# Placing TensorE's weight operands by their byte address modulo 128 in a one-core encoder layer

## Chip, cores, metric

The kernel runs on one core of a Trainium2 chip, as a single launch. The metric is device time in microseconds, the median of three runs. Work is spread over the engines TensorE (PE; its weight loads are listed apart, as PEld), VectorE (DVE), ScalarE (ACT), GpSimd (POOL) and the DMA queue of SyncE (SP).

## What is computed

One layer of a hybrid encoder, for 512 positions of 1024 channels in float32. One projection feeds eight differential attention heads and a bidirectional Mamba-2 scan of 16 heads in four groups; both results are concatenated and projected back, and a SwiGLU block follows, each with a residual and a layer norm:

```python
h = jnp.einsum('bsd,de->bse', x, w_in[l])
q, k, v, z, xbc, dt_raw = jnp.split(h, splits, axis=-1)
attn_out = diff_attention(q, k, v, ...)
ssd_out = ssd_mixer(z, xbc, dt_raw, ...)
mix = jnp.einsum('bse,ed->bsd', jnp.concatenate([attn_out, ssd_out], axis=-1), w_out[l])
x = layernorm(DEEPNORM_ALPHA * x + mix, ln1_g[l], ln1_b[l])
hid = jax.nn.silu(jnp.einsum('bsd,df->bsf', x, w_gate[l])) * jnp.einsum('bsd,df->bsf', x, w_up[l])
ffn = jnp.einsum('bsf,fd->bsd', hid, w_down[l])
x = layernorm(DEEPNORM_ALPHA * x + ffn, ln2_g[l], ln2_b[l])
```

## The kernel before

Every large product is made in three float32r products: each operand is split into a rounded part `h` and a remainder `l`, and `mm3` (L174 to L179) adds h·h, h·l and l·h in one PSUM bank. `product` (L883 to L887) does the same in the gate and up stage. In a call `T.matmul(o, a, b)` the operand `a` is **stationary** (128 columns, loaded into the array ahead of the matmul: the PEld row) and `b` is **moving** (256 or 512 columns, streamed through it).

**The weight chunks.** The weights lie in HBM as 130 chunks of [128, 1024] float32. `wload` (L96) fetches a chunk by DMA into a tile of tag `raw`; `wprep` (L101) makes its parts, `h` on ACT (L106) and `l` on DVE (L107), in tiles `wh` and `wl` of the pool `wp`, which has three buffers a tag. `wget` (L110) calls it two chunks ahead. Chunks 0 to 23 are the scan's projections in four groups of six (the last two of six are z), 24 to 47 the attention's in four groups of six (the first two are v), 48 to 63 the output projection (`I_OUT`), 64 to 107 gate and up (`I_FF`), 108 to 129 down (`I_DN`).

**Stages in order of time, by the trace.** Scan projections and scan (to about 220 us): `col_units` (px, pB, pC: weights stationary, 512 columns of x moving) and `row_units` (z: x stationary, 256 columns of weights moving). Attention (about 220 to 450 us): q and k by `col_units`, v by `row_units`, woven between the steps of the heads by hand-written counts. Output projection `wo` (to about 528 us; 512 columns of weights moving, the mix tiles stationary); its last four chunks are kept in tiles `hold` of the pool `hw` by `tile_major` (L764). Gate and up: the first tiles whole (`ff_mm`, 256 columns), then Winograd's 2 x 2 form over 20 pairs (about 553 to 747 us): of its seven products of 12 matmuls the two of `p_1` and `p_2` have a weight chunk's own tiles `wh`, `wl` as stationary operands (rows `M<-x1h,wh` and `C<-x1h,wh`), the other five have sums and parts that `halves` makes in the pool `fp` (S1 to S4, A22). Down projection `dn` (to the end): weights moving, the split `hid` tiles (`hid_split`, L1006) stationary; its last sequence tile goes in two banks of 256 columns, `dn13x` and `dn13ps`, and its last four chunks are kept in tiles `keep`, in the place of x.

Order on each engine is the order of the code, with a few pieces held back by `tc.issue_after`; a tile's next use waits until its readers are done.

**Where operands lie.** Every row of an operand that a matmul uses begins at the tile's byte address in the partition plus a multiple of 128 bytes, so the address modulo 128 is the same for all slices of a tile. In the built program it is 96 for x, x1, T1 to T3, mix and all `wh`, `wl`; 32 for S1 to S4, A22 and `hold`; `keep` has 96; the split `hid` tiles have 96 in three rotating buffers (`dnr`) and 32 in the pool `dn` and in the first tile. 'Near' below means that the two operands of a matmul have the same address modulo 128, 'far' that they differ by 64.

Of the kernel before, what the change touches and what calls it, by code (L numbers as in the profile page):

```python
# [8 lines left out]
F32 = mybir.dt.float32  # L9
R32 = mybir.dt.float32r  # L10
# [3 lines left out]
P = 128  # L14
# [14 lines left out]
I_OUT = N_IN  # L29
I_FF = I_OUT + 16  # L30
I_DN = I_FF + 2 * FT
# [19 lines left out]
def encoder(ctx, tc, xt, xs, wall, wdt, consts, masks, vecs, pvec, lnv, out):  # L51
# [21 lines left out]
    def weave(steps, units, counts):  # L73
        """Emits steps in order with counts[i] of the units after step i, and the remaining units at the end."""
        done = 0
        for f, n in zip(steps, counts, strict=True):
            f()
            for u in units[done:done + n]:
                u()
            done += n  # L80
        for u in units[done:]:
            u()

# [1 line left out]
    cst = cp.tile([P, N_C], F32, name="cst")  # L85
# [6 lines left out]

    wcache = {}
    AHEAD = 2

    def wload(i):  # L96
# [4 lines left out]
    def wprep(i, raw=None, h=None, l=None):  # L101
        raw = wload(i) if raw is None else raw
        if h is None:
            h = wp.tile([P, 1024], R32, tag="wh", name=f"wh{i}")
            l = wp.tile([P, 1024], R32, tag="wl", name=f"wl{i}")
        A.copy(h, raw)  # L106
        V.tensor_tensor(l, raw, h.bitcast(F32), op=ALU.subtract)  # L107
        wcache[i] = (h, l)
# [6 lines left out]

# [1 line left out]
    xh = xtp.tile([P, KT, S], R32, tag="xh", name="xh")  # L117
# [63 lines left out]
    def col_units(i, name, done, step=2):  # L181
        """x @ w for 128 columns, transposed: [columns, 512]; then done(psum)."""
        st = {}

        def unit(k0):
            if k0 == 0:
                st["o"] = bank("mm", name)
                st["w"] = [w.rearrange("p (k c) -> p k c", k=KT) for w in wget(i)]
            h, l = st["w"]
            mm3(st["o"], [(h[:, k], l[:, k], xh[:, k], xl[:, k]) for k in range(k0, k0 + step)],  # L190
                first=k0 == 0, last=k0 + step == KT)
            if k0 + step == KT:
                done(st["o"])
        return [lambda k0=k0: unit(k0) for k0 in range(0, KT, step)]

    def row_units(i, name, tag, done):
        """x @ w for 256 columns: two banks of [128 positions, 2, 256]; done(half, psum)."""
        st = {}

        def unit(tp, tt, kh):  # L200
            if (tp, tt, kh) == (0, 0, 0):
                w0, w1 = wget(i, 2), wget(i + 1, 1)
                st["w"] = [[w.rearrange("p (k c) -> p k c", k=4) for w in ww] for ww in (w0, w1)]
            if (tt, kh) == (0, 0):
                st["o"] = bank(tag, f"{name}{tp}")
            t = 2 * tp + tt
            sl = slice(t * P, (t + 1) * P)
            h, l = st["w"][kh]
            mm3(st["o"][:, tt * 256:(tt + 1) * 256],
                [(xh[:, 4 * kh + k, sl], xl[:, 4 * kh + k, sl], h[:, k], l[:, k]) for k in range(4)],  # L210
                first=kh == 0, last=kh == 1)
            if (tt, kh) == (1, 1):
                done(tp, st["o"])
        return [lambda a=(tp, tt, kh): unit(*a) for tp in range(2) for tt in range(2) for kh in range(2)]

# [1 line left out]
    sps = ExitStack()  # L217
# [27 lines left out]

# [1 line left out]
    dtv = ep.tile([P, 2, NT, NH], F32, name="dtv")  # L247
# [4 lines left out]
    sel = msk[:, M_SEL:M_SEL + 256].rearrange("p (a k) -> p a k", a=2)  # L252
    # per direction d: rows erow[d] carry the exponents, the other 64 rows the mask
    erow = (slice(0, 64), slice(64, 128))
# [115 lines left out]

    # stationary parts of the exponents per direction and half of the columns, in the last mix tiles' places
    lhsC = [[mxp[0].tile([P, NT, P], R32, tag=f"m{q}{14 + d}", name=f"lhsC{d}{q}") for q in "hl"] for d in range(2)]
# [6 lines left out]

    # mix^T in two float32r parts: 16 tiles of [128 channels, 512]  # L380
    mixh, mixl = [None] * 16, [None] * 16
# [6 lines left out]

# [1 line left out]
    bc = lambda a, n: a[:, :, None].broadcast_to([a.shape[0], 4, n])  # L390
# [124 lines left out]

# [1 line left out]
    va, qk = {}, {}  # L517
# [31 lines left out]

# [1 line left out]
    late = []  # L551
# [18 lines left out]

# [1 line left out]
    mxp[0] = mxs.enter_context(tc.tile_pool(name="mxa", bufs=1, side="right"))  # L572
# [72 lines left out]

# [1 line left out]
    def pair(i, ahead=None):  # L647
        return [w.rearrange("p (k c) -> p k c", k=2) for w in wget(i, ahead)]

    def outer_units(i0, order, lhs, acc, n0, n1, total):  # L650
        """acc(t) += lhs tiles (pairs in order) x weight chunks i0 + n0 .. i0 + n1 - 1."""
        st = {}

        def unit(c, i):
            if i == 0:
                st["w"] = pair(i0 + c)
            h, l = st["w"]
            eh, el = lhs(2 * order[c] + i)
            for t in range(NT):
                sl = slice(t * P, (t + 1) * P)  # L660
                for b, o, w in acc(t):
                    mm3(b, [(eh[:, sl], el[:, sl], h[:, i, o:o + w], l[:, i, o:o + w])],
                        first=c == 0 and i == 0, last=c == total - 1 and i == 1)
        return [lambda c=c, i=i: unit(c, i) for c in range(n0, n1) for i in range(2)]
# [34 lines left out]

# [1 line left out]
    fx = ctx.enter_context(tc.tile_pool(name="fx", bufs=1))  # L701
    xr = fx.tile([P, NT, D], F32, tag="res", name="xr")

    def ln_consts(pool, i):
        r = []
        for j in (i, i + 1):
            r.append(pool.tile([P, D], F32, tag=f"ln{j}", name=f"ln{j}"))
            nc.gpsimd.dma_start(r[-1], lnv[j][None, :].broadcast_to([P, D]))  # L708
        return r
# [54 lines left out]
    def tile_major(i0, order, lhs, acc, done, hold, after):  # L764
        """As outer_units, with the last NHELD chunks resident and used one sequence tile at a time."""
        n = len(order)
# [21 lines left out]
    acc1 = [[(bank("ps", f"wo1{t}"), 0, 512)] for t in range(NT)]  # L788
    with tc.tile_pool(name="hw", bufs=1) as hw:
        ln1 = ln_consts(hw, 0)  # L790
        tile_major(I_OUT + 8, OUT_ORDER, mix, acc1.__getitem__, done1,
                   lambda j: [hw.tile([P, 1024], R32, tag=f"{q}{j}", name=f"hold{q}{j}") for q in "hl"],
                   lambda: wget(I_FF))
    mxs.close()

# [1 line left out]
    hidp = ctx.enter_context(tc.tile_pool(name="hid", bufs=1, side="right"))  # L797
# [11 lines left out]

    # Winograd's 2 x 2 form: operands from x1^T's blocks B (k half, sequence half)  # L810
    def block(i, j):
# [16 lines left out]
    def t_steps(q):  # L828
        """x1^T of sequence tile 2 + q, and the operands that come of it."""
        b12, b22 = x1t(2 + q, 0), x1t(2 + q, 1)  # L830
# [12 lines left out]

    # operands from the weight blocks of two column tiles: A11 A12 / A21 A22 (columns, k half)
    ops, mats = {}, {}
# [50 lines left out]
    def put(j, f, c, src):  # L896
        """One block of gate (silu) or up (times gate) into hid."""
        d = hid_tile(f)[:, c]
        if j % 2 == 0:
            A.activation(d, src, AF.Silu)  # L900
        else:
            V.tensor_tensor(d, d, src, op=ALU.mult)
# [42 lines left out]

    # the first two tiles of gate and up, whole; sequence half 0 of three chunks first
    def ff_w(f, w):
# [50 lines left out]

# [1 line left out]
    NEARLY = 1  # L1000
# [5 lines left out]
    def hid_split(e, ph):  # L1006
        """hid tile e in two parts; the later tiles' parts stay for both column halves."""
        key = e if e >= NRING else (ph, e)
# [39 lines left out]
    ffs.close()  # L1048
    dn = ctx.enter_context(tc.tile_pool(name="dn", bufs=1))
    ln2 = ln_consts(dn, 2)  # L1050
    for f in units[NMORE:]:
# [93 lines left out]
```

## Time and profile before

| | |
|---|---|
| median of 3 runs | 878.93 us (878.69 to 879.1) |
| span of the profiled execution, first to last instruction | 876.8 us |
| mean granted TensorE clock over the span | 0.997 |
| PE busy | 862.4 us, 98% |
| PEld busy | 748.6 us, 85% |
| DVE busy | 616.6 us, 70% |
| ACT busy | 457.7 us, 52% |
| POOL busy | 121.3 us, 14% |

The profile gives the profiled execution's own time as its span; the median of the runs is 2.1 us above it, and those 2.1 us lie around the span. The busy share of an engine is an average over stages. A row of PE is a matmul from its start to its modelled end; matmuls overlap, so the row's duration is longer than the distance from one start to the next. In a steady stream that distance (here: the pace) is what a matmul costs, and the chain of waits shows it as the length of a run of matmuls divided by their count.

### The profile page before, as it was taken

To read this page: it belongs to the slowest core of one execution; us is meant where nothing else is said; L and a number is where in the kernel's file an instruction comes from. 1 tells how busy PE (TensorE), PEld (TensorE's weight loads), DVE (VectorE), ACT (ScalarE), POOL (GpSimd) and SP (SyncE) were. 2 spreads that over 40 slices of the span, in tenths; PEclk is the share of its full clock that TensorE was granted. 3 is DMA by queue.
4 is the path that set the end of the run, shared out by engine and by line. 5 is a ranking of instruction groups with operands and counts; after the bars stand their busy time and mean duration, and the time that the engine had idled before them with its cause. 6 is when DMAs were issued, how large, how long until landed. Compare 5 with 4: busy or idle time off the path is not lost.

```text
span 876.8 us, 13791 instructions
## 1 busy us (share of the span) xinstructions
PE 862.4 (98%) x5404; PEld 748.6 (85%) x5404; DVE 616.6 (70%) x1071; ACT 457.7 (52%) x893; POOL 121.3 (14%) x137
## 2 busy tenths in 40 slices
PE   7999999999999999999999999999999999999996
PEld 3888989899778687786788889999999999888885
DVE  4978788786567666766644579988888887733617
ACT  4777776667456555655632314555555555621500
POOL 3025252535400000000000023000000000000002
PEclk9999999999999999999999999999999999999999
DMA  7321212112212103111135600343233233332402
GB/s 259 113 96 49 73 50 80 66 49 70 76 49 72 50 25 96 50 49 49 49 109 186 209 25 25 112 129 98 96 123 118 98 116 133 112 96 96 145 1 96
DMA packets 23008, 78.74 MB, mean 90 GB/s; under 512 B 2688, under 2 KB 2944, under 8 KB 22944
## 3 DMA queue, kind: packets, MB, share of 16 engines
q1 hardware_dynamic: 22320, 75.60, 25.8%
q0 software_dynamic: 624, 2.27, 0.8%
q8 instruction: 42, 0.69, 0.3%
q14 instruction: 22, 0.18, 0.1%
HBM read 75.77 MB, written 2.10 MB: 89 GB/s over the span
## 4 chain that ended last, share of the span: by engine, by line
PE 67%; DVE 4%; ACT 1%; issue 1%; DMA 0%; POOLq 0%; POOL 0%; DVEq 0%; ACTq 0%
PE M L887 12%; PE N L887 6%; PE dn L178 4%; PE dn L177 4%; PE dn L179 4%; PE wo L177 3%; PE wo L178 3%; PE wo L179 3%; PE C L887 3%; PE o L618 3%; PE s L592 2%; PE s L590 2%; PE at L606 1%; PE v L177 1%; PE k L177 1%; PE q L177 1%
## 5 line engine op out<-in xcount | busy, mean ns | idle before, releaser
L107 DVE TENSOR_TENSOR wl<-wr,wh 128x1024 fp32r<-128x1024 f32 x101 | 124.5, 1233 | 66.8 <-ACT wh L106 63.5
L106 ACT CAST wh<-wr 128x1024 fp32r<-128x1024 f32 x101 | 105.7, 1049 | 77.6 <-PE wo L179 28.6
L598 ACT ACTIVATE ss<-ss,mn 128x512 f32<-128x512 f32 x64 | 46.0, 720 | 25.9 <-DVE mn L595 25.8
L595 DVE CUSTOM_DVE_ANT_0 ss<-s,tab 128x512 f32<-128x512 f32 x64 | 43.2, 688 | 16.4 <-PE s L592 15.8
L178 PE MATMUL dn<-wl,hidh 128*128 128x512 f32 x130 | 51.0, 392 | 0.0
L177 PE MATMUL dn<-wh,hidh 128*128 128x512 f32 x130 | 50.9, 392 | 0.0
L179 PE MATMUL dn<-wh,hidl 128*128 128x512 f32 x130 | 50.6, 389 | 0.0
L893 ACT COPY e<-M 128x256 f32<-128x256 f32 x60 | 22.4, 372 | 43.1 <-PE M L887 43.0
L456 ACT ACTIVATE rE<-vals,msk 64x128 fp32r<-64x128 f32 x128 | 43.0, 391 | 1.0 <-DVE vals L339 0.4
L177 PE MATMUL wo<-wh,mixh 128*128 128x512 f32 x96 | 38.3, 399 | 0.0
L177 PE MATMUL v<-wh,xh 128*128 128x256 f32 x128 | 37.8, 296 | 0.0
L178 PE MATMUL wo<-wl,mixh 128*128 128x512 f32 x96 | 37.6, 392 | 0.0
L179 PE MATMUL wo<-wh,mixl 128*128 128x512 f32 x96 | 37.5, 390 | 0.0
L179 PE MATMUL v<-wh,xl 128*128 128x256 f32 x128 | 36.7, 286 | 0.0
L177 PE MATMUL z<-wh,xh 128*128 128x256 f32 x128 | 36.4, 286 | 0.0
L178 PE MATMUL v<-wl,xh 128*128 128x256 f32 x128 | 36.3, 284 | 0.0
L179 PE MATMUL z<-wh,xl 128*128 128x256 f32 x128 | 36.2, 283 | 0.0
L178 PE MATMUL z<-wl,xh 128*128 128x256 f32 x128 | 36.2, 283 | 0.0
L618 PE MATMUL o<-va,as 128*128 128x128 f32 x256 | 34.0, 275 | 0.1
L724 POOL TENSOR_TENSOR rs<-rs,mhalf 128x1 f32<-128x1 f32 x8 | 12.2, 1525 | 158.6 <-DVE rs L723 158.6
L708 POOL DMA_DIRECT2D ln<-in_lnv x4 | 2.3, 580 | 227.1 <-PE dn L178 208.8
L618 PEld LDWEIGHTS o<-va,as 128*128 128x128 f32 x256 | 31.6, 192 | 0.7 <-ACT osq L621 0.3
(355 smaller groups left out, 2926.6 us busy)
## 6 DMA issues: line engine op xcount, KB each, us to landing
wr<-in_wall SPq DMA_DIRECT2D x130, 512.0 KB, 3.5
xraw<-in_xt SPq DMA_DIRECT2D x8, 256.0 KB, 6.8
xr<-in_xs SPq DMA_DIRECT2D x4, 512.0 KB, 6.3
ln<-in_lnv POOLq DMA_DIRECT2D x4, 512.0 KB, 4.4
out_y<-xr SPq DMA_DIRECT2D x8, 256.0 KB, 2.0
msk<-in_masks SPq DMA_DIRECT2D x1, 490.0 KB, 5.7
cst<-in_consts SPq DMA_DIRECT2D x1, 448.0 KB, 6.7
vec<-in_vecs POOLq DMA_DIRECT2D x1, 168.0 KB, 5.9
```

The source lines that it names most:

```text
L106: A.copy(h, raw)
L107: V.tensor_tensor(l, raw, h.bitcast(F32), op=ALU.subtract)
L177: T.matmul(o, ah, bh, start=first and i == 0, stop=False)
L178: T.matmul(o, ah, bl, start=False, stop=False)
L179: T.matmul(o, al, bh, start=False, stop=last and i == n - 1)
L456: A.activation(r[d][e, h], vals[e, sls[t]], AF.Copy, scale=hmask[e, 4 * g + h:4 * g + h + 1])
L590: T.matmul(sbs[c], QS[:, c, sl], KS[:, c], start=True, stop=False)
L595: V.tensor_tensor_reduce(out=s, in0=sb, in1=tab[:, 384 - 128 * t:896 - 128 * t], scale=1.0, scalar=3.0e38, op0=ALU.add, op1=ALU.min, accum ...
L598: A.activation(s, s, AF.Exp, scale=-1.0, bias=mn[:, t, c:c + 1], accum_out=Z[:, t, c:c + 1])
L618: T.matmul(o, ats[t][:, kt * P:(kt + 1) * P], vv[:, kt, j * P:(j + 1) * P], start=kt == 0, stop=kt == NT - 1)
L887: T.matmul(o, x[:, k], y[:, k], start=first and n == 0, stop=last and n == 11, skip_group_check=True)
L893: mats[j]["i" + name] = A.copy(e, src)
```

## The change

`wh` and `wl` become six tags of one buffer each, used in rotation (`nW`), in tiles of 1040 elements (4160 bytes, 64 more than a multiple of 128). A chunk takes 1024 of them, from element 0 or 16, so that both of its parts lie at 32 modulo 128 where `wfar` says 1 and at 96 where it says 0. `wfar` is 1 for the z chunks, the v chunks and gate and up. Two pads of 64 bytes, `hpad` and `dpad`, move what follows in the pools `hw` and `dn`: `hold` and the later split `hid` tiles go from 32 to 96.

```diff
-    wcache = {}
+    wcache, nW = {}, [0]
...
+    def wfar(i):
+        if i < 24:
+            return int(i % 6 in (4, 5))
+        if i < I_OUT:
+            return int((i - 24) % 6 in (0, 1))
+        return int(I_FF <= i < I_DN)
...
         if h is None:
-            h = wp.tile([P, 1024], R32, tag="wh", name=f"wh{i}")
-            l = wp.tile([P, 1024], R32, tag="wl", name=f"wl{i}")
+            n = nW[0] % 3
+            nW[0] += 1
+            h, l = (wp.tile([P, 1040], R32, tag=f"w{q}{n}", name=f"w{q}{i}", bufs=1)[:, o:o + 1024]
+                    for q, o in (("h", 16 * wfar(i)), ("l", 16 - 16 * wfar(i))))
...
     with tc.tile_pool(name="hw", bufs=1) as hw:
+        hw.tile([P, 16], F32, name="hpad")
...
     dn = ctx.enter_context(tc.tile_pool(name="dn", bufs=1))
+    dn.tile([P, 16], F32, name="dpad")
```

The matmuls whose operands' addresses modulo 128 change (moving, stationary), counted in the two built programs:

| matmuls | count | columns | before | after |
|---|---|---|---|---|
| z | 384 | 256 | 96, 96 | 32, 96 |
| v | 384 | 256 | 96, 96 | 32, 96 |
| gate and up, `p_1` and `p_2` (M, C by `wh`, `wl`) | 480 | 256 | 96, 96 | 96, 32 |
| gate and up, first tiles (`ff`) | 144 | 256 | 96, 96 | 96, 32 |
| dn13x, dn13ps with later `hid` tiles | 72 | 256 | 96, 32 | 96, 96 |
| wo with `hold` | 96 | 512 | 32, 96 | 96, 96 |
| dn with later `hid` tiles (72 of them by `keep`) | 252 | 512 | 96, 32 | 96, 96 |

All other matmuls keep theirs, and so do the `raw` tiles. The order of the instructions on every engine, and what each waits for, are the same in the two programs: 5,125 matmuls, the same DMAs, casts and subtracts.

## Rows read from the trace of the kernel before

**Rows 1.** The page, part 1: each engine over the whole span.

```profile
## 1 busy us (share of the span) xinstructions
PE 862.4 (98%) x5404; PEld 748.6 (85%) x5404; DVE 616.6 (70%) x1071; ACT 457.7 (52%) x893; POOL 121.3 (14%) x137
```

**Rows 2.** Waits of PE, longest first: who, in total, times, longest.

```profile
PE dps L148 <- POOL warm L146: 2.5, 1, 2.5
PE ff L178 <- DVE x1l L747: 1.1, 1, 1.1
```

**Rows 3.** The chain of waits, 580.5 to 591 us: start, length, what.

```profile
582.09 1.44 PE C L887 x12
583.53 2.72 PE M L887 x24
586.25 2.72 PE N L887 x24
```

**Rows 4.** Busy time in the gate and up stage: PE, PEld, DVE, ACT, POOL, PEclk.

```profile
553.40:747.00 193.60, 193.24 (x1666) 192.71 (x1665) 166.57 (x258) 110.48 (x185) 0.00 (x0) 1.00 0.35 115
```

**Rows 5.** PE groups by line and shape (total, mean ns, idle before), 256 columns.

```profile
L887 PE MATMUL C<-x1h,wh 128*128 128x256 f32 x80 | 22.6, 283 | 0.0
L887 PE MATMUL N<-x1h,S3h 128*128 128x256 f32 x80 | 22.1, 276 | 0.0
L887 PE MATMUL M<-x1l,A22h 128*128 128x256 f32 x80 | 22.1, 276 | 0.0
L177 PE MATMUL z<-wh,xh 128*128 128x256 f32 x128 | 36.4, 286 | 0.0
L178 PE MATMUL v<-wl,xh 128*128 128x256 f32 x128 | 36.3, 284 | 0.0
L179 PE MATMUL ff<-x1h,wl 128*128 128x256 f32 x48 | 13.6, 283 | 0.0
```

**Rows 6.** The tile dn13ps: min/median/max ns of its loads and matmuls.

```profile
L177 PEld LDWEIGHTS dn13ps<-wh,hidh x14: 187/192/192, 810.5 to 846.5; 128*128 128x128 f32 x14
L177 PE MATMUL dn13ps<-wh,hidh x14: 276/283/283, 810.6 to 846.6; 128*128 128x256 f32 x14
L177 PEld LDWEIGHTS dn13ps<-keeph,hidh x8: 187/188/188, 866.0 to 868.4; 128*128 128x128 f32 x8
L177 PE MATMUL dn13ps<-keeph,hidh x8: 276/276/276, 866.1 to 868.5; 128*128 128x256 f32 x8
```

**Rows 7.** The tile e on PE: 256 columns, moving at 64, stationary at 96.

```profile
L460 PE MATMUL e<-rE,lhsC1l x16: 278/279/294, 54.8 to 216.1; 128*128 128x256 f32 x16
```

**Rows 8.** The chain of waits, 248 to 256 us.

```profile
249.63 0.70 DVE QS L538
253.17 0.59 ACT KS L545
```

**Rows 9.** The chain of waits, 530 to 556 us.

```profile
545.78 1.21 DVE wl L107
550.66 3.48 DMA wr<-in_wall
```

**Rows 10.** Tiles holdh, wh, hidh, hidl: 512-column matmuls, min/median/max ns.

```profile
L177 PE MATMUL wo<-holdh,mixh x32: 394/394/478, 503.4 to 526.9; 128*128 128x512 f32 x32
L177 PE MATMUL wo<-wh,mixh x96: 387/389/499, 425.5 to 502.7; 128*128 128x512 f32 x96
L177 PE MATMUL dn<-keeph,hidh x24: 388/388/388, 846.9 to 862.7; 128*128 128x512 f32 x24
L178 PE MATMUL dn<-keepl,hidh x24: 392/392/392, 847.1 to 862.9; 128*128 128x512 f32 x24
L179 PE MATMUL dn<-keeph,hidl x24: 394/394/394, 847.4 to 863.2; 128*128 128x512 f32 x24
```

**Rows 11.** ACT groups that write the operands.

```profile
L106 ACT CAST wh<-wr 128x1024 fp32r<-128x1024 f32 x101 | 105.7, 1049 | 77.6 <-PE wo L179 28.6 <-PE dn L179 26.4 <-PE q L178 7.2
L853 ACT CAST S1h<-Sa 128x1024 fp32r<-128x1024 f32 x20 | 21.1, 1053 | 8.8 <-PE N L887 5.2 <-DVE Sa L815 3.2 <-ACT A22h L853 0.4
```

## The prediction, made before the changed kernel ran

> **What bounds the kernel now.** I read the engines' totals first, then PE's waits, then the chain of waits stage by stage, and last the PE groups by shape and single tiles. PE is busy for 98% of the span; of the other engines DVE comes next with 70% [rows 1]. PE's waits are few: the longest are 2.5 us at the very start and 1.1 us at the first gate and up tile [rows 2]. So PE's own stream sets the end, and what shortens a matmul's pace shortens the kernel, except where the chain leaves PE.
>
> The pace is the thing to see. In the Winograd stage the chain shows 12 matmuls C in 1.44 us, 120 ns each, and right behind them 24 matmuls M and 24 N in 2.72 us each, 113.3 ns [rows 3]. All have 128 stationary and 256 moving columns, at a granted clock of 1.00, the upper level of 2.4 GHz [rows 4]. The groups say the same in durations: 283 ns for C with `wh` as stationary operand, 276 for N with S3 and for M with A22 [rows 5]. A duration is the pace plus a constant 163, so differences of durations are differences of pace. The 120 goes with near operands (96, 96), the 113 with far ones (96, 32). z, v and ff, all near, stand at 283 to 286 as well [rows 5].
>
> That it is the address and not the tile shows in dn13ps. There the same `wh` tiles are streamed against `hid` parts, of which ten uses are near and four far: 276 at the least, 283 in the median; with `keep` against far parts all eight are 276 [rows 6]. The weight loads move alike, 192 ns near and 187 to 188 far [rows 6]. I read it so: a near pair's load and stream disturb each other, the load takes longer than a stream of 256 columns, and the pace becomes the load's.
>
> **The change, part by part.** The gain per moved matmul of 256 columns is 120 less 113.3, 6.7 ns.
>
> *Gate and up, p_1 and p_2.* 480 x 6.7 ns = 3.2 us. These go from (96, 96) to (96, 32), the very pair that the neighbouring products have [rows 3, 5]. The stage is PE's: 193.24 of 193.60 us busy, and DVE, the next, 166.57 [rows 4]; 3.2 us less leaves DVE at 87% of the stage. All of it counts.
>
> *z.* 384 x 6.7 = 2.6 us. Here the weights are the moving operand, and the new pair is (32, 96), which no matmul of 256 columns has in this trace. The bounds: 113.3 if only the distance matters, and 131 by the slowest of the e matmuls, 256 columns at (64, 96), which take 279 ns in the median and 294 at most, 18 above the far 276 [rows 7]. I take 113.3, since dn13ps is the nearest: weights streamed, 256 columns, and a distance of 64 in it is enough [rows 6].
>
> *v.* Again 384 x 6.7 = 2.6 us with the same bounds. The first head's softmax holds PE: from 249.63 us the chain runs through DVE and ACT, past 253 us [rows 8]. I take off 0.3 us for what waits there anyway, 2.3 us.
>
> *ff.* 144 x 6.7 = 0.96 us, but beside other work: in that stretch the chain lies on DVE and a DMA of 3.48 us, not on PE [rows 9], and PE waits 1.1 us for x1l between these matmuls [rows 2]. I count 0.3 us.
>
> *dn13x and dn13ps.* 72 matmuls go the other way, far to near, 276 to 283 [rows 6], and 48 of them are the last of the kernel: + 72 x 6.7 = + 0.5 us.
>
> *hold.* 96 matmuls of 512 columns go from (32, 96), 394 ns in the median, to the pair of the other wo, 389 [rows 10]: -0.5 us. They lead into the layer norm's chain, so this shifts all that follows.
>
> *dn.* 252 matmuls of 512 columns go from far to near. Far ones, by `keep`, take 388, 392 and 394 ns in turn, 391.3 in the mean; near ones, for which the nearest row is wo by `wh`, 389 [rows 10]. 252 x 2.3 = -0.6 us.
>
> *At no cost.* ACT and DVE write the same number of elements to addresses 64 bytes off. ACT's cast took 1049 ns to `wh` at 96 and 1053 to S1 at 32 [rows 11]. Most of it lies beside PE; if all 101 were 4 ns longer and uncovered it would be 0.4 us. The tags with one buffer each give the rotation that three buffers of one tag gave; instructions and waits are the same, so no queue is passed.
>
> The sum: -3.2 - 2.6 - 2.3 - 0.3 + 0.5 - 0.5 - 0.6 = -9.0 us. Against the profiled execution it makes a span of 867.8 instead of 876.8; the 2.1 us around it stay, and the median goes from 878.93 to **869.9 us**.
>
> **The rivals.**
>
> *The placement is neutral.* 120 and 113 would then belong to how the products are scheduled, not to addresses, and moving the chunks would give 878.9 us. For it speaks that all near groups of the Winograd stage use freshly prepared chunks. Against it speaks dn13ps, where one tile shows both values with nothing else changed [rows 6]. 5%. The Trainium skill's page "TensorE: Matmul & The Clock Gate", section "Step-by-step: what each phase is for", states this rival's rule: it gives PE two independent read ports, so that loading the next weights takes no read bandwidth from the running matmul. By that rule the change is worth nothing and the time is 878.9; the 7 ns between near and far in this trace do not agree with it.
>
> *Moving the streamed operand does not help.* z and v then stay at 120, and only gate and up, hold and dn change: 3.2 + 0.3 - 0.5 + 0.5 + 0.6 = 4.1 us, **874.8 us**. For it: the one pair (32, 96) of the trace, hold, is at 394 the slowest of the steady 512-column pairs, while (96, 32) has 388 to 394 [rows 10]; so the two directions may not be alike. Against: at 512 columns even the good direction gains nothing, so these rows say little of 256. 12%, values in between included.
>
> *(32, 96) is worse than near.* This one ends slower. If z and v ran like the slowest e, at 131, the 768 would lose 11 ns each, 8.4 us, against 4.1 gained elsewhere: **883.2 us**. It decides from a pace of 120 + 4100 / 768 = 125.3 ns on. For it: e's 294 and hold's 394 [rows 7, 10]. Against: e's median, 279, lies between far and near. 3%.
>
> *Waits take part of it.* If v within the heads (288), z of the first group (96) and ff give nothing because DVE and ACT hold the next step, 1.6 + 0.6 + 0.3 = 2.5 us fall away: 872.4 us. Rows 8 and 9 show that the chain leaves PE at such places, rows 2 that it seldom does. 10%.
>
> That the change doesn't do what it says I leave out: the addresses stand in the built program.
>
> **How the numbers follow.** The forecast, 869.9 us, has 70%. Its own least time is with v and ff counted in full, 1.0 us lower, and another 2 ns off each of the 252 dn matmuls, 0.5 us: 868.4. Upwards the range takes in lost waits and the rival in which z and v gain nothing, to 875.0. Neutral and worse are left out. A measurement of this kernel can tell about 0.2% from no change, 1.8 us. Forecast, waits and the streamed-operand rival are all faster by more: 0.92. Neutral is within it: 0.05. The worse pair is slower: 0.03.
>
> **What would show it.** Right: C and M by `wh`, z, v and ff at 276 instead of 283, their weight loads at 188 instead of 192; dn13ps by `keep` at 283; wo by `hold` at 389; the chain with 12 C in 1.36 us; order and waits as before. Wrong: z and v at 283 or more with C at 276 (the streamed side), all of them at 283 (neutral), or all at 276 with a span over 870 and PE waits in the heads that are not there now.

## The result: 0.6% slower, and the profile after

The changed kernel takes **883.7 us** (median of 4 runs, 883.31 to 885.39) beside 878.84 for the kernel before (4 runs, 878.69 to 879.1): a ratio of 1.0057, 95% interval 1.0043 to 1.0071. I had predicted 869.9 us, in a range from 868.4 to 875.0, and 0.92 for faster. The profiled execution below is the run of 885.39 us (span 883.5); 1.7 us of its surplus lies ahead of 21 us, where the granted clock of the page's first slice is lower (digit 8, before it 9); the other three runs take 883.31 to 883.70. From 21 us on the traces differ by 4.9 us, which is what the medians differ by.

The engines over the whole span, kernel after (answers to [rows 1]):

```profile
PE 868.5 (98%) x5404; PEld 751.3 (85%) x5404; DVE 617.0 (70%) x1071; ACT 456.8 (52%) x893; POOL 121.2 (14%) x137
```

PE's busy time grew by 6.1 us with the same 5,404 instructions; DVE and ACT did not move by a microsecond. PE's waits, kernel after (answers to [rows 2]; who, in total, times, longest):

```profile
PE dps L159 <- POOL warm L157: 2.5, 1, 2.5
...
PE ff L189 <- DVE x1l L758: 1.1, 1, 1.1
PE M L899 <- ACT e L905: 0.7, 1, 0.7
```

No wait is longer than before by more than 0.3 us, so no wait took the place of anything: the matmuls themselves are slower. The chain of waits from 580 to 591 us, kernel after (answers to [rows 3]):

```profile
581.20 2.83 PE M L899 x24
584.03 1.41 PE C L899 x12
...
588.26 2.83 PE N L899 x24
```

C by the chunk went from 1.44 to 1.41 us for 12, 117.5 ns each and not 113.3. The other products, which the change was not to touch, went from 2.72 to 2.83 us for 24: 117.9 ns each. The gate and up stage in the same stretch of time, kernel after (PE, PEld, DVE, ACT, POOL, PEclk; answers to [rows 4]), still is PE's at a granted clock of 1.00:

```profile
553.40:747.00 193.60, 192.91 (x1633) 192.46 (x1632) 165.26 (x254) 107.67 (x180) 0.00 (x0) 1.00 0.32 110
```

1,633 matmuls fit where 1,666 did. The PE groups by line and shape, kernel after (total, mean ns, idle before; answers to [rows 5]):

```profile
L188 PE MATMUL z<-wh,xh 128*128 128x256 f32 x128 | 36.0, 282 | 0.0
L189 PE MATMUL v<-wl,xh 128*128 128x256 f32 x128 | 35.9, 280 | 0.0
...
L899 PE MATMUL N<-x1h,S3h 128*128 128x256 f32 x80 | 22.4, 280 | 0.0
L899 PE MATMUL C<-x1h,wh 128*128 128x256 f32 x80 | 22.4, 280 | 0.0
L899 PE MATMUL M<-x1l,A22h 128*128 128x256 f32 x80 | 22.3, 279 | 0.0
L190 PE MATMUL ff<-x1h,wl 128*128 128x256 f32 x48 | 13.4, 280 | 0.0
```

Everything stands at 279 to 282: what had 283 to 286 gained 3 or 4 ns instead of 7, and what had 276 lost 3 or 4. Between near (120 ns) and far (113.3 ns) there is a third pace, 117 to 118 ns. It is in the kernel before too: there T1 by S1, far in both lines, has 279 ns in the first of the 20 pairs and 276 from the second on (four matmuls each, min/median/max ns, first to last start):

```profile
L887 PE MATMUL N<-T1h,S1h x4: 279/279/279, 557.7 to 558.8; 128*128 128x256 f32 x4
...
L887 PE MATMUL N<-T1h,S1h x4: 276/276/276, 568.1 to 569.1; 128*128 128x256 f32 x4
```

So one product, at unchanged addresses modulo 256, can run at either pace. Single tiles of the kernel after (min/median/max ns; answers to [rows 6, 10]):

```profile
L188 PEld LDWEIGHTS dn13ps<-keeph,hidh x8: 192/192/192, 872.6 to 875.1; 128*128 128x128 f32 x8
L188 PE MATMUL dn13ps<-keeph,hidh x8: 283/283/283, 872.7 to 875.2; 128*128 128x256 f32 x8
...
L188 PE MATMUL wo<-holdh,mixh x32: 390/393/477, 505.0 to 528.3; 128*128 128x512 f32 x32
...
L188 PE MATMUL wo<-wh,mixh x96: 390/397/499, 426.0 to 504.3; 128*128 128x512 f32 x96
...
L188 PE MATMUL dn<-keeph,hidh x24: 387/389/389, 853.5 to 869.1; 128*128 128x512 f32 x24
```

dn13ps by `keep` and dn by `keep` went where I had put them (283 and 389). `hold` gained 1 ns instead of 5. wo by `wh`, whose addresses modulo 128 didn't change at all, went from 389 to 397.

Where the time went, stage by stage, as the distance between the starts of the same two matmuls in both traces (us against the kernel before; the last three columns are versions that come below):

| stage (time in the trace of before) | after | e8 | e9 | e14 |
|---|---|---|---|---|
| scan part, 21 to 196, without the next row | +0.2 | +0.3 | +0.2 | -0.2 |
| z of groups 1 to 3 (88, 136, 183) | -0.7 | -1.1 | -0.7 | -0.6 |
| v and attention, 196 to 448 | -0.6 | -0.7 | -0.6 | -1.0 |
| wo by chunks, 448 to 503 | +1.0 | +1.0 | +1.0 | 0.0 |
| wo by `hold`, 503 to 528 | -0.1 | -0.5 | -0.1 | -0.5 |
| first tiles of gate and up, 528 to 553 | -0.1 | -0.5 | -0.4 | -0.5 |
| Winograd part, 553 to 745 | **+4.3** | -2.3 | -2.7 | -2.5 |
| dn, 745 to 866 | +1.0 | +1.5 | +1.1 | -0.2 |
| sum | +4.9 | -2.3 | -2.2 | -5.4 |

The Winograd part is the loss, and it can be counted: 1,200 matmuls of the five products by S, A22 and T lose some 4.5 ns, 5.4 us, and 480 by the chunk gain some 2.3, 1.1 us: +4.3.

### The profile page after: what moved, and what is told of

Read it like the earlier page. It is cut to its first block, busy times and chain, and to the rows that moved or that the text cites. A ratio compares the mean times of both kernels' runs of the same rounds, so it can differ in the third digit from the quotient of the medians.

```text
span 883.5 us, 13791 instructions
## 1 busy us (share of the span) xinstructions
PE 868.5 (98%) x5404; PEld 751.3 (85%) x5404; DVE 617.0 (70%) x1071; ACT 456.8 (52%) x893; POOL 121.2 (14%) x137
## 4 chain that ended last, share of the span: by engine, by line
PE 67%; DVE 4%; issue 1%; ACT 1%; DMA 0%; POOLq 0%; POOL 0%; DVEq 0%; ACTq 0%
PE M L899 13%; PE N L899 6%; PE dn L188 4%; PE dn L190 4%; PE dn L189 4%; PE wo L188 3%; PE wo L189 3%; PE wo L190 3%; PE o L629 3%; PE C L899 3%; PE s L603 2%; PE s L601 2%; PE at L617 1%; PE q L188 1%; PE k L188 1%; PE q L189 1%
```

## The experiments

What the diff moves besides the residues modulo 128 stands in the built programs. Six tiles of 4160 bytes instead of 4096 put the six chunk buffers at different places modulo 256, and they push all that is allocated behind them on that side (x, x1, S, A22, `hold`, the split `hid` of the pool `dn`) up by 384 bytes, while T, mix and `hid` on the other side stay. Modulo 128 that is nothing; modulo 256 it is a shift by 128. Addresses modulo 256 in the gate and up stage:

| kernel | x1 | S, A22 | T | chunks (h and l) |
|---|---|---|---|---|
| before | 224 | 160 | 224 | 224 |
| after | 96 | 32 | 224 | 32, 160, 32 by buffer |
| e1 | 96 | 32 | 224 | h 224, 96, 224; l 96, 224, 96 |
| e4 | 96 | 32 | 224 | h as after; l 96, 224, 96 |
| e5 | 224 | 160 | 224 | 32 |
| e6, e10 | 96 | 32 | 224 | 224 |
| e7 | 224 | 160 | 224 | h and l as e4 |
| e8 | 224 | 160 | 224 | 32, 160, 32 |
| e9 | 96 | 32 | 96 | 32, 160, 32 |
| e11, e12 | 224 | 160 | 224 | 224 |
| e13 | 224 | 160 | 224 | 160 |
| e14 | 224 | 160 | 224 | 32 |

e2 has the addresses of the kernel after, and e3 those of e1. I began with two theories. **A**: a far stream has two paces, 113 and 118; which one it takes is left over from the matmuls before it, and the near groups C and M, which the change removed, brought it back to 113. **B**: 118 belongs to the new addresses of x1, S and A22. The first three runs undo the far placement in parts and leave the tiles where the change has them.

**e1_all_near.**

```diff
     def wfar(i):
-        if i < 24:
...
-        return int(I_FF <= i < I_DN)
+        return 0
```

> The changed kernel with the placement rule returning 0 everywhere: all weight chunks at 96 modulo 128, near their partners as before, but in the new tiles and with both pads, so that x, S and A22 lie 384 bytes higher, as in the changed kernel. Theory A (the pace of a far pair depends on the state that the matmuls before it leave in TensorE: behind a near, load-bound run it is 113 ns, without one the stream stays at 118): the products with S and A22 go back to 113 ns, C and M by wh stay at 120, z and v at 120, and the time is 877 to 879.5 us. Theory B (118 belongs to the new absolute addresses of x1, S and A22): the products with S and A22 stay at 118 with C at 118 to 120, and the time is 883 to 886 us.

883.22 us, ratio 1.0049 (1.0034 to 1.0064). The Winograd part is 2.6 us longer than before: `near` chunks bring the others back only in part (T1 by S1 averages 115 ns, x1 by S 118), so A in its plain form falls. C by the chunk now takes 118.4 or 119.1 ns a matmul, depending on the buffer, and not 120: with the spacing of 4160, 'near' modulo 128 is a distance of 0 or 128 modulo 256.

**e2_gate_up_far** and **e3_z_v_far**: far only for gate and up, and only for z and v.

```diff
     def wfar(i):
-        if i < 24:
-            return int(i % 6 in (4, 5))
-        if i < I_OUT:
-            return int((i - 24) % 6 in (0, 1))
         return int(I_FF <= i < I_DN)
```

> The changed kernel with the rule true for gate and up alone; z and v near. Theory A: nothing in the Winograd stage resets the stream, all its products are at 118 as in the changed kernel (about +4.3 us in that stage), z and v at 120: 883 to 885.5 us. Theory B: the same. A third theory (C, z and v carry the loss into later stages): the Winograd stage is at 113 throughout and the time falls below 876 us.

```diff
     def wfar(i):
...
-        return int(I_FF <= i < I_DN)
+        return 0
```

> The changed kernel with the rule true for z and v alone; gate and up near. Theory A: C and M by wh at 120, the products with S and A22 at 113 as before, z and v at 114 to 118 as in the changed kernel (1.2 us gained by 447 us of the span): 876.5 to 879 us. Theory B: S and A22 at 118: 882 us or more.

884.91 us (1.0069, 1.0052 to 1.0086) and 882.64 us (1.0045, 1.003 to 1.006). With z and v near the Winograd part still loses 3.5 us, and with gate and up near it loses 2.8, so neither half of the far placement is what costs. e2 has every address of the kernel after in that part, which loses 4.3 there; its profiled run is the shortest of four (884.03 to 885.21), so the 0.8 us between them may lie in the run.

**e4_h_far_l_near.** Only the parts `h` follow the rule, `l` is always near.

```diff
-                    for q, o in (("h", 16 * wfar(i)), ("l", 16 - 16 * wfar(i))))
+                    for q, o in (("h", 16 * wfar(i)), ("l", 16)))
```

> The changed kernel with the remainder l near (96) and the rounded part h far (32) wherever the rule is true, so that every third matmul of z, v, ff and the products by wh and wl is near. Theory A: the near third runs at 120 and resets the stream, the far two thirds and all products with S and A22 run at 113: 768 + 624 matmuls gain two thirds of 6.7 ns, 6 us, and the time is 872 to 875 us. Theory B: S and A22 at 118, 882 us or more.

882.45 us (1.0038, 1.0024 to 1.0051). The chain of waits of e4, 640 to 649 us:

```profile
639.90 1.42 PE M L899 x12
641.32 1.41 PE C L899 x12
642.74 2.77 PE M L899 x24
645.51 2.78 PE N L899 x24
```

Runs of 24 hold two products, and 2.77 us is one at 113.3 and one at 117.5: the products by A22, T1 and T3 are back at 113 while T2 and x1 by S stay at 118, with all their addresses as in the kernel after. B in its plain form, a fixed price of an address, falls too: only the chunks' `l` moved, and what other matmuls do next to a pair has a say.

The next four separate the two side effects of the tile size, spacing and shift.

**e5_all_far_4096.** The kernel before, its buffers spaced by 4096 as they were, all chunks 64 bytes up, everything behind them 512 up.

```diff
         if h is None:
+            if not wcache:
+                wp.tile([P, 16], F32, tag="pad0", name="pad0", bufs=1)
             h = wp.tile([P, 1024], R32, tag="wh", name=f"wh{i}")
             l = wp.tile([P, 1024], R32, tag="wl", name=f"wl{i}")
+            if not wcache:
+                wp.tile([P, 112], F32, tag="pad1", name="pad1", bufs=1)
```

> The kernel before, whose wh and wl tiles keep their spacing of 4096 bytes and all move up by 64, with x, S and A22 moved by 512: every pair that stood at a distance in the kernel before stands at the same one modulo 512, except those with a weight chunk, which are all 64 off. Theory A (a far stream has two paces, 113 and 118 ns; a disturbance puts it at 118 and only near pairs bring it back): after the waits around 556 us the Winograd stage runs at 118 to its end, 882 to 885 us. Theory D (118 comes from tile distances that the new spacing and the shift of 384 bytes changed modulo 512): all of it at 113, z and v too: 868 to 872 us.

**e6_shift_384.** The kernel before with nothing but 384 unused bytes behind the chunk buffers.

```diff
             l = wp.tile([P, 1024], R32, tag="wl", name=f"wl{i}")
+            if not wcache:
+                wp.tile([P, 96], F32, tag="pad1", name="pad1", bufs=1)
```

> The kernel before with an unused tile of 384 bytes behind the weight tiles and nothing else: x, S and A22 lie 384 higher, all residues modulo 128 as before, the distances of x and S to wh, T and mix changed by 384. Theory A alone: near is near modulo 128, C and M by wh at 120 and the rest at 113, 878 to 880 us. Theory D: the distances modulo 512 count, so that this alone gives most of the loss, 881.5 to 884 us, with products by S at 114 to 118.

e5 takes 877.15 us (0.9981, 0.9972 to 0.9991), between the two forecasts: from the second pair on all products of the Winograd part run at 113.3, C and M by the chunk among them, 3.0 us less than before, but z and v stay at 118. e6 takes 884.83 us (1.0071, 1.0056 to 1.0086): 384 bytes that nobody uses cost 6 us, 4.2 of them in the Winograd part. Two tiles of e6 (min/median/max ns, first to last start):

```profile
L889 PE MATMUL C<-x1h,wh x80: 279/280/285, 556.6 to 743.7; 128*128 128x256 f32 x80
...
L889 PE MATMUL M<-T2h,S1h x80: 276/281/281, 558.0 to 746.5; 128*128 128x256 f32 x80
```

C's first and last start lie 187.1 us apart, exactly as in the kernel after (556.1 to 743.2), and 183.1 in the kernel before (554.8 to 737.9). The shift alone keeps the part at the third pace, without one chunk moved.

**e7_h_far_l_near_512** and **e8_after_512**: e4 and the kernel after, each with 128 unused bytes more, so that x, x1, S and A22 lie 512 bytes off their old places instead of 384.

```diff
+        if nW[0] == 3:
+            wp.tile([P, 32], F32, tag="wpad", name="wpad", bufs=1)
         A.copy(h, raw)
```

> The kernel with h far and l near, with another 128 bytes behind the weight tiles, so that x, S and A22 have moved by 512 and stand to T, mix and hid as before modulo 512. Theory D: T2 by S and x1 by S, at 118 in the run without these 128 bytes, fall to 113: 2 x 240 x 4.3 ns = 2 us less, 879 to 881 us, and what 512-column matmuls had lost by the shift comes back, another 1 to 2 us. Theory A alone: no change from that run, 882 to 883 us.

> The changed kernel with another 128 bytes behind the weight tiles: x, S and A22 stand to T, mix and hid as in the kernel before modulo 512, and the chunks are far as in the changed kernel. Theory A: the Winograd stage has no near pair, stays at 118: 881 to 884 us. Theory D: the products by S return to 113 and C and M reach it: 869 to 874 us.

e7 takes 884.74 us (1.0069, 1.0054 to 1.0084), e8 877.16 us (0.998, 0.997 to 0.999). The same pad makes one version 2.3 us slower and the other 6.5 us faster, and both times lie outside what either theory forecast. In e8 the products start at 113, run at 118 from the end of the first pair through the second, and at 113 from the third on, and no near matmul is between them; with it falls the part of A by which only near pairs bring the stream back. Two tiles of e8:

```profile
L901 PE MATMUL C<-x1h,wh x80: 276/276/280, 553.3 to 734.2; 128*128 128x256 f32 x80
...
L901 PE MATMUL M<-T2h,S1h x80: 276/276/280, 554.7 to 736.9; 128*128 128x256 f32 x80
```

What remained was **D**: the distance of two operands counts further than modulo 128. The next four runs ask whose distance, and modulo what.

**e9_T_moved_too.** The kernel after with 128 unused bytes in the pool of T1 to T3, on the other side of the memory. x1, S, A22 and the chunks keep the changed kernel's addresses; only T moves.

```diff
     Tops["T4"] = Bs[0][1]
+    tp_.tile([P, 32], F32, name="tpad")
```

> The changed kernel with one unused tile of 128 bytes in the pool of T1, T2, T3, which moves these six tiles down by 128 bytes, as many as x1, S and A22 lie off their distance to T modulo 512; x1, S, A22, the chunks, mix and hid stay where the change put them. Theory D1 (the distance between T and S, A22, x1 modulo 512 decides): the products by T come back to a start every 113 ns from the fourth pair on as before, and as the pace is carried from product to product, the others too; the Winograd part gives back some 6.5 us, the kernel takes about 877. Theory D2 (the absolute addresses of x1, S and A22 modulo 512 decide, whatever T does): every product stays at 117 to 118 ns and the kernel at 883 to 884. A rival between them: T's products alone come back (48 of every 72 matmul groups are not by T), some 2 us, 881 to 882.

876.71 us (0.9979, 0.997 to 0.9988): 7.0 us less than the kernel after. The chain of waits of e9, 580 to 591 us:

```profile
581.57 1.36 PE C L900 x12
582.92 2.72 PE M L900 x24
585.64 2.72 PE N L900 x24
```

and tiles of e9:

```profile
L900 PE MATMUL M<-T2h,S1h x80: 276/276/276, 555.7 to 737.5; 128*128 128x256 f32 x80
...
L900 PE MATMUL M<-x1h,A22h x80: 276/276/279, 563.7 to 745.0; 128*128 128x256 f32 x80
...
L900 PE MATMUL N<-x1h,S3h x80: 276/276/280, 566.4 to 748.5; 128*128 128x256 f32 x80
```

This is the run that settles where the loss comes from. The products by T came back, and with them x1 by A22, x1 by S and C and M by the chunk, whose two operands lie byte for byte where they lay in the kernel after, at 280. So the absolute addresses of x1, S and A22 are out as the cause (theory D2), and what counts is where T lies beside them: products whose own pair is unchanged go along with it. x1, S and A22 move together in every run, so no run tells T's distance to S, its own partner, from T's distance to x1, the other moving operand of the stream.

**e10_shift_128, e11_shift_256, e12_shift_512**: e6 with the unused tile at 32, 64 and 128 elements.

```diff
-                wp.tile([P, 96], F32, tag="pad1", name="pad1", bufs=1)
+                wp.tile([P, 32], F32, tag="pad1", name="pad1", bufs=1)
```

> The kernel before with only an unused tile of 128 bytes behind the chunk buffers: x1, S, A22, hold and the later tiles on the left move by 128 bytes, the chunks keep their places and their spacing of 4096. Theory D (distances modulo 512 decide): the Winograd products run at 117 to 118 ns as with 384 bytes, 4 to 6 us more, about 883 to 885. Rival (384 is a bad place, not every place other than a multiple of 512): products at 113, 879.

> As e10, with 256 bytes. If the rule goes modulo 256, the products stay at 113 ns and the time at 879 as before; if it goes modulo 512, they run at 117 to 118 and the time is 883 to 885.

> As e10, with 512 bytes: the control. Theory D: nothing moves modulo 512, the products by S, A22 and T at 113, C and M by the chunk at 120, the time of the kernel before within 0.1 per cent (878 to 879.7). If it is under 878, part of what the two versions at 877.2 gained came from the 512 bytes and not from the chunks; if it is 883 or more, theory D falls.

| shift | median us | ratio to before |
|---|---|---|
| 128 | 884.41 | 1.0069 (1.0052 to 1.0086) |
| 256 | 878.91 | 1.0 (0.9991 to 1.001) |
| 384 | 884.83 | 1.0071 (1.0056 to 1.0086) |
| 512 | 878.72 | 0.9999 (0.999 to 1.0009) |

Shifts of 128 and 384 lose and shifts of 256 and 512 don't, so for this loss the rule goes modulo 256. Open was the other part of the error: why z and v gained so little, and why wo by the chunks lost. For this I built a version in which all six buffers lie at the same place modulo 256, near at a distance of 0, far 64 below or 64 above, with a total shift of 768 bytes for x1 (512 for S and A22). For its room the statistics of the layer norms move to other pools (`fpad` and the larger `dpad` keep what follows at its place).

**e13_far_below_256** and **e14_far_above_256**.

```diff
-            h, l = (wp.tile([P, 1040], R32, tag=f"w{q}{n}", name=f"w{q}{i}", bufs=1)[:, o:o + 1024]
-                    for q, o in (("h", 16 * wfar(i)), ("l", 16 - 16 * wfar(i))))
+            h, l = (wp.tile([P, c], R32, tag=f"w{q}{n}", name=f"w{q}{i}", bufs=1)[:, o:o + 1024]
+                    for q, c, o in (("h", 1072, 48 * wfar(i)), ("l", 1040, 16 - 16 * wfar(i))))
...
-    st6 = fx.tile([P, NT, 4, 6], F32, name="st6")
+    s6 = [mxs.enter_context(tc.tile_pool(name="s6", bufs=1, side="right")).tile([P, NT, 4, 6], F32, name="st6")]
+    fx.tile([P, 32], F32, name="fpad")
...
-    dn.tile([P, 16], F32, name="dpad")
+    s6.append(dn.tile([P, NT, 4, 6], F32, name="st6b"))
+    dn.tile([P, 48], F32, name="dpad")
```

> The changed kernel with all six chunk buffers at the same place modulo 256: near is x's place (224), far is 64 bytes below it (160), and the shift behind the chunks comes to 768 bytes, for which the statistics tile of the first norm moves to the other side. T, x1, S, A22 have the distances of the kernel before. Theory D256 (each pair's own distance modulo 256): near chunks at 0, so the wo part is back at the time of before (the 1.0 us goes); z and v with the chunk 64 below the stationary x run at 113 ns in every buffer, so each z group gives 0.8 to 0.9 us instead of 0.25, the v products (196 to 225 us and the attention part) 1.5 to 2.3; C and M at 113, the Winograd part 3 us shorter than before; hold 0.5 shorter; dn within 0.7 either way. In all about 871, between 870 and 873. Rival (only modulo 128 matters for the chunks, and z's small gain has another cause): z groups at -0.25 to -0.4 each, wo unchanged from the changed kernel, some 876.

and e14 with the two sizes exchanged:

```diff
-                    for q, c, o in (("h", 1072, 48 * wfar(i)), ("l", 1040, 16 - 16 * wfar(i))))
+                    for q, c, o in (("h", 1040, 16 * wfar(i)), ("l", 1072, 48 - 48 * wfar(i))))
```

> The same with far 64 bytes above x's place (32 modulo 256). Theory D256: wo as before; z and v pairs, with the chunk 64 above the stationary x, run at 118 ns in every buffer (z groups -0.2 each, v -0.6 in all); C and M at 113 as in the version with all chunks 64 off at a spacing of 4096; about 874.5, between 873 and 876. Rival (the sign does not matter, only that it is 64 off): the same time as the version with far below, within 0.5 us.

e14 takes **873.52 us** (ratio 0.9942, 0.9929 to 0.9954), as expected, and is the fastest of all: it beats the kernel before by 5.2 us and the changed one by 10.2. e13 takes 880.2 us (1.0017, 1.0008 to 1.0026), and there the expectation failed. Up to the Winograd part the two differ by 0.3 us; then e14 gains 2.5 in the Winograd part and e13 loses 4.3. The chain of waits of e13, 640 to 649 us:

```profile
641.21 2.83 PE M L900 x24
644.04 2.83 PE N L900 x24
```

and of e14, 580 to 591 us:

```profile
580.98 2.72 PE M L900 x24
583.70 2.72 PE N L900 x24
586.42 2.72 PE M L900 x24
589.14 1.36 PE C L900 x12
```

In e13 T, S, A22 and x1 have the distances modulo 256 of the kernel before, where they run at 113.3, and the chunk lies 64 below x1 like S and A22: every pair of the part is (224, 160). Yet all run at 118, while in e14 x1 by the chunk, at a distance of 192, runs at 113.3. So theory D256, by which each pair's own distance sets its pace, falls, although its forecast for e14 came true. What e13 loses is the way back. T1 by S1 in its first pair and in its second, and PE's wait between them (tile N, waits; kernel e13):

```profile
L900 PE MATMUL N<-T1h,S1h x4: 276/276/276, 555.2 to 556.2; 128*128 128x256 f32 x4
...
L900 PE MATMUL N<-T1h,S1h x4: 280/280/280, 566.1 to 567.2; 128*128 128x256 f32 x4
...
PE M L900 <- ACT e L906: 0.8, 1, 0.8
```

The part starts at 113 in e13 as in e14 and e8, chunk products included; after PE's wait of 0.8 to 1.1 us in the first pair all three are at 118. e14 is back at 113 within four matmuls of the next chunk product, whose stationary operand lies at 32 where S lies at 160. e8 passes the second pair, whose chunk lies at 160, without a change and is back with the third, at 32. In e13 every chunk lies at 160, and the stream stays at 118 for some 190 us. That a product at another place than S brings the stream back is a reading of these three traces; no run tests it, and in e7, whose `h` lies at 32 in two buffers of three, the stream does not come back.

Tiles of e14:

```profile
L188 PE MATMUL wo<-wh,mixh x96: 387/389/499, 423.9 to 501.1; 128*128 128x512 f32 x96
...
L188 PE MATMUL wo<-holdh,mixh x32: 387/389/487, 501.8 to 524.7; 128*128 128x512 f32 x32
...
L189 PE MATMUL z<-wl,xh x128: 279/279/282, 41.2 to 194.7; 128*128 128x256 f32 x128
```

wo by the chunks is back at 389 and `hold` stands at 389 too: at 512 columns a distance of 0 modulo 256 is the good one, and near modulo 128 was not enough. z stays at 279.

**What stays open.** Which placements let the stream return to 113 I can't derive. e4 (a shift of 384, `l` near) has three of its products at 113 in spite of a distance of 192 from T to S, and e7 (a shift of 512, the same chunks) has all at 118 in spite of 64. And z: in e8 the distances between starts are 113 to 114 ns in the buffer that lies 64 below x and 118 in the one 64 above, but in e13, where every buffer lies 64 below, they are 118 as well but for the end of the third group. I tried no placement that runs z and v at 113 throughout, and don't know whether there is one.

## Why the prediction was wrong

By the terms of its sum (us), against the kernel after and against e14, where the side effects are gone:

| term | forecast | after | e14 |
|---|---|---|---|
| gate and up, `p_1` and `p_2` | -3.2 | -1.1, and +5.4 beside it | -2.5, whole stage |
| z (measured: the last three of its four groups) | -2.6 | -0.7 | -0.6 |
| v (measured: the stage from 196 to 448) | -2.3 | -0.6 | -1.0 |
| ff | -0.3 | -0.1 | -0.5 |
| hold | -0.5 | -0.1 | -0.5 |
| dn13x, dn13ps, dn (to 866 us; behind it both lose 0.2 more) | -0.1 | +1.0 | -0.2 |
| not in the sum: wo by chunks | 0 | +1.0 | 0.0 |
| not in the sum: 21 to 196 without z of groups 1 to 3 | 0 | +0.2 | -0.2 |

- **The step that failed** is the paragraph "At no cost". It counted the six tags and their tiles only by the casts' time and the order, and put their effect on all other matmuls at nothing because these keep their addresses modulo 128. They do, but their distances modulo 256 they don't: the larger tiles move x1, S and A22 by 384 bytes against T, and the buffers against each other. The first is 4.3 us in the Winograd part where I had -3.2, and e6 and e9 show it from both sides: unused bytes alone cost 6 us, moving T along gives back 7.0. The second is the 1.0 us of wo (e6, with the old spacing, loses 0.1 there). In dn, at +1.0 us, both take part: e6 with the shift alone loses 1.1, e8 with the spacing alone 1.5, e14 with neither gains 0.2.
- **The mechanism of the main term was half right.** Far from x1, C and M by the chunk can run at 113.3 (e5, e9, e14), as the products by S and A22 did [rows 3]; e5 and e14 gain 3.0 and 2.5 us there. But being 64 apart modulo 128 does not hold a matmul at 113.3: in e13 all of them are, and run at 118. Of three paces I knew two, and read each as the price of a pair. The third stood in the trace of before, in the first pair above, and I didn't look there; with 113 and 120 alone a change from near to far could not lose. The reading that a near pair's load becomes the pace is tested by no run.
- **z and v were mis-sized**, 4.9 us forecast and 1.6 got in e14: there the streamed operand moved by 64 brings 120 to 118 for the most part, not to 113. Of the bounds I took for (32, 96) I chose the gainful end by dn13ps [rows 6]; the rival in which "moving the streamed operand does not help" gave 874.8, and e14, without the side effects, stands at 873.5. It was the better forecast of the placement as such, and had 12%.
- **dn13ps and dn by `keep`** came out as sized, 283 against 276 and 389 in place of 388 to 394 [rows 6, 10]. The half microsecond of `hold` came where `hold` lies at mix's place modulo 256 (e7, e8, e13, e14) and not in the kernel after, where it lies 128 off; e6 and e10, with `hold` 64 above mix, gain 0.4 of it, so near is not needed for it.
- **The rivals.** "Neutral" falls in e5: chunks moved by 64 at the same spacing run at 113. The Trainium skill's page "TensorE: Matmul & The Clock Gate", section "Step-by-step: what each phase is for", gives that rival its rule, that a weight load takes no read bandwidth from the running matmul. No run here looks at the read ports, but the rule does not foresee what these traces show: matmuls of one form have 276, 280 or 283 ns by where operands lie and what ran before, at a granted clock of 1.00. The slower rival's 883.2 beside the measured 883.7 is luck: its mechanism was that z and v lose, and they gained a little. The rival of waits falls by PE's waits above.
- Of what I named as showing the prediction wrong, "all at 276 with waits", "z and v at 283", "all at 283", none is what came: C, M, ff, v and S's products all at 279 to 280, z at 282.

## What to carry to other kernels

When an edit changes a tile's size, list every tile that is allocated behind it, and compare where the operands of all matmuls lie modulo 256 before and after, not only those of the tile that was edited. A pad of 128 bytes that brought the total shift to a multiple of 256 cost no time and was worth 6.5 us of 880 in e8; but it is no guarantee, for e7 and e13 have such shifts too and take 884.7 and 880.2. A run with the pad alone (e6, e12) tells a placement from its side effect. And a pace is no property of a pair of tiles: the same pair runs at 113 or 118 by what ran before and around it, so look at the first matmuls of a stage, and behind each wait of PE, before a pace is taken for the price of an address.

## What the runs showed of the hardware

- Matmuls of 256 moving columns in float32r, at the upper clock level, have three paces: 113.3, 117 to 118 and 120 ns, with rows of 276, 279 to 281 and 283 ns. The weight loads beside them take 187 to 188 ns at 113.3 and 192 at 120 [rows 6]; in e13, at 118, they take 187 to 188 as well, so a load does not tell 118 from 113.
- Which of 113 and 118 a pair runs at is a state of the stream: T1 by S1 has 279 and then 276 ns in the kernel before, 276 and then 280 in e13, and a state lasts for up to 190 us. In e8, e13 and e14 it turned from 113 to 118 at a wait of PE of 0.8 to 1.1 us.
- Where operands lie modulo 256 sets which state lasts: an unused tile that shifts x1, S and A22 by 128 or 384 bytes costs 5.6 and 6.0 us, one by 256 or 512 nothing within 0.1%, and T shifted along gives 7.0 us back (e9).
